# Values of the meta tokens from one stationary operand of 64 columns, in the bank of the first value tile

## The chip, the cores and the metric

The kernel runs on one core of a Trainium2 chip. The metric is the device time of one execution in microseconds, taken as the median over runs. A profiled execution has its own time and a trace with every instruction of the engines: TensorE (PE; its weight loads are listed as PEld), VectorE (DVE), ScalarE (ACT), GpSimd (POOL), and SyncE (SP), which issues DMAs.

## What is computed

One decoder layer on 256 tokens with 16 learned meta tokens ahead of them (272 keys). From the normalised input one projection gives queries, a latent of 256 numbers for each token, an indexer and gates. Each query attends to its top 68 keys. The part that matters here, cut from the reference:

```python
c_kv = rms_norm(c_kv, kv_norm_g[l])
q_lat = jnp.einsum('bthe,hce->bthc', q, w_uk)
...
sel = c_kv[batch_ix, idx]
s = jnp.einsum('bqhr,bqkr->bqhk', ql, sel).astype(jnp.float32) * (HEAD_DIM ** -0.5)
...
p = jax.nn.softmax(s, axis=-1).astype(sel.dtype)
return jnp.einsum('bqhk,bqkr->bqhr', p, sel)
...
o = jnp.einsum('bthc,hce->bthe', o_lat, w_uv)
```

The kernel makes keys (latent times w_uk) and values (latent times w_uv) for each of 16 heads instead, masks the keys that were not chosen, and multiplies. After the attention come the output projections, the merge with a pooling branch, and the MLP.

## The kernel before

Every fp32 factor is split into two parts, hi (rounded, made by ACT) and lo (the rest, made by DVE or, for half of some weights, by POOL). A product takes three matmuls: hi times hi, hi times lo, lo times hi. Weights stream in blocks; the cast of a block's weights (L239, ACT) and its lo parts (L242 on DVE and POOL) are written three blocks ahead of their matmuls. Every engine runs its instructions in the order of the program.

`kv_block(m)`, for m = 0 to 7, is one such weight block and makes keys and values of heads 2m and 2m+1. Eight of them are inserted among the blocks of the input projection; the text calls them blocks 0 to 7. Each made five PSUM banks of the pool `m` in turn: the keys of each head (`mm3`, L147 to L149, split by L112 on ACT and L113 on DVE), then the values of the meta tokens, of tokens 0 to 127 (v0) and of tokens 128 to 255 (v1), each with six matmuls (L626 to L628: two halves of the latent, three products). v0 and v1 are split by L112 and L113. The pool `m` has three banks, so the fourth and fifth users wait until the first and second have been read.

The values of the meta tokens are kept as four strips of 32 partitions in one tile `vm`: hi (L631, ACT), hi again, lo (L632, DVE), hi again (L635, two ACT copies behind L632). The probabilities of the meta tokens lie in the same way in `pm`: hi in partitions 0 to 15, lo in 32 to 47, hi in 64 to 79, zeros elsewhere (L700, L701, L703). One matmul of 128 partitions, L715, then adds the three products at once; the fourth strip of `vm` meets zeros.

The attention of a head is a queue of small steps, one popped ahead of each weight block: scores (`s1`, 6 matmuls, L147 to L149 on q and k), then `s4` (L715 and the products with v0 and v1) with the exponentials, then `s3` (transposes L692 to L697, then the splits into `pt` and `pm`) with the normalisation (L683, L684). A score step mostly stands right behind a kv block. Where a slab of output columns ends, four banks of the pool `g` (five banks) are emptied by ACT (L133) and DVE (L134), and the next slab's matmuls L305 need them.

Of the kernel before, what the change touches and what calls it, by code (L numbers as in the profile page):

```python
# [9 lines left out]
F32 = mybir.dt.float32  # L10
F32R = mybir.dt.float32r
AF = mybir.ActivationFunctionType
ALU = mybir.AluOpType
# [3 lines left out]
P = 128  # L17
D = 2048
KC = D // P
S = 256  # L20
NM = 16
# [50 lines left out]
def flat(slot):  # L72
    return slot.rearrange("p a b -> p (a b)")
# [4 lines left out]
def decoder_layer(ctx, tc, x, meta, g_mix, w_in, kv_g, ik_g, w_uk, w_uv, w_ao, w_pool,  # L78
                  pool_scale, w_po, w_out, g_mlp, w1, w2, g_fin, out):
    nc = tc.nc  # L80
    x, out, w_in, w_ao, w_po, w_out, w1, w2 = x[0], out[0], w_in[0], w_ao[0], w_po[0], w_out[0], w1[0], w2[0]
# [12 lines left out]
    ecst = early.enter_context(tc.tile_pool(name="ecst", bufs=1))  # L94
# [4 lines left out]
    slots = Slots(act, NSLOT, F32R, "r")  # L99
    plain = Slots(fpl, NPLAIN, F32, "f")  # L100
    V, A, T, G = nc.vector, nc.scalar, nc.tensor, nc.gpsimd
# [6 lines left out]
    def mbank():  # L108
        return pm.tile([P, 512], F32, tag="m", name="m")

    def split_psum(dst, ps, n, rows=P):
        A.copy(dst[:rows, 0, :n], ps)  # L112
        V.tensor_tensor(out=dst[:rows, 1, :n], in0=ps, in1=dst.bitcast(F32)[:rows, 0, :n], op=ALU.subtract)  # L113

    def split_sbuf(dst, src, n):
        A.copy(dst[:, 0, :n], src)
        V.tensor_tensor(out=dst[:, 1, :n], in0=src, in1=dst.bitcast(F32)[:, 0, :n], op=ALU.subtract)
# [28 lines left out]
    def mm3(ps, wh, wl, xh, xl, first, last):  # L146
        T.matmul(ps, wh, xh, start=first, stop=False)  # L147
        T.matmul(ps, wh, xl, start=False, stop=False)  # L148
        T.matmul(ps, wl, xh, start=False, stop=last)  # L149
# [41 lines left out]
    def add_unit(load, halves):  # L191
        u = {"load": load, "left": len(halves)}
        for src, shape, mm, pops in halves:
            blocks.append(Block(u, src, shape, mm, pops))
        return blocks[-len(halves)]
# [55 lines left out]
    def push(fn, ready=None):  # L251
        side.append((fn, ready))
# [134 lines left out]
        return hT[k], NM  # L387

    kvraw, ckv, qi, kw = {}, [], [], {}
    wn = [cst.tile([P, IH], F32, name=f"wn{t}") for t in range(2)]  # L390

    def split_heads(dst, ps):
# [22 lines left out]
    def push_kv_norm():  # L415
        env = {}

        def s0():
            kvf = kvraw["t"]
            for cc in range(2):  # L420
                V.tensor_tensor(out=kvf[:, cc, :], in0=kvf[:, cc, :], in1=rbc, op=ALU.mult)

        def s1():
            env["sq"] = plain.get()
            A.activation(flat(env["sq"]), flat(kvraw["t"]), AF.Square)

        def s2():
            ps = mbank()
            sq = env["sq"]
            for cc in range(2):  # L430
                T.matmul(ps[:, 0:L], ones, sq[:, cc, :], start=cc == 0, stop=cc == 1)
            env["r"] = plain.get()
            V.tensor_scalar(env["r"][:, 0, :], ps[:, 0:L], 1.0 / R, EPS, op0=ALU.mult, op1=ALU.add)

        def s2b():
            A.activation(env["r"][:, 0, :], env["r"][:, 0, :], AF.Sqrt)

        def s2c():
            V.reciprocal(env["r"][:, 0, :], env["r"][:, 0, :])

        def s3():
            kvf = kvraw["t"]
            for cc in range(2):
                V.scalar_tensor_tensor(out=kvf[:, cc, :], in0=kvf[:, cc, :], scalar=gcol[:, 40 + cc:41 + cc],
                                       in1=env["r"][:, 0, :], op0=ALU.mult, op1=ALU.mult)

        def s4():
            kvf = kvraw["t"]
            for cc in range(2):
                t = slots.get()  # L450
                split_sbuf(t, kvf[:, cc, :], L)
                ckv.append(t)
            for k in ("sq", "r"):
                plain.put(env[k])
            plain.put(kvraw["t"])

        for f in (s0, s1, s2, s2b, s2c, s3, s4):
            push(f)
# [144 lines left out]
    vP = {}  # L603

    def kv_block(m):
        def load(raw):
            for kind, w in ((0, w_uk), (1, w_uv)):
                nc.sync.dma_start(out=raw[:, kind * 512:(kind + 1) * 512].rearrange("p (a e) -> p a e", e=DH),
                                  in_=w[2 * m:2 * m + 2].rearrange("h (c p) e -> p (h c) e", p=P))

        def go(hi, lo):
            hi = hi.rearrange("p k (h c e) -> p k h c e", h=2, c=2)
            lo = lo.rearrange("p k (h c e) -> p k h c e", h=2, c=2)
            for h in range(2):
                ps = mbank()[:, 0:L]
                for c in range(2):
                    mm3(ps, hi[:, 0, h, c], lo[:, 0, h, c], ckv[c][:, 0, :], ckv[c][:, 1, :], c == 0, c == 1)
                kT[2 * m + h] = slots.get()
                split_psum(kT[2 * m + h], ps, L)
            vv = []  # L620
            for o, rows in ((0, NM), (NM, P), (NM + P, P)):
                ps = mbank()[:, 0:S]
                pv = ps.rearrange("p (h e) -> p h e", h=2)
                for c in range(2):
                    ch, cl = ckv[c][:, 0, o:o + P], ckv[c][:, 1, o:o + P]
                    T.matmul(pv, ch, hi[:, 1, :, c], start=c == 0, stop=False)  # L626
                    T.matmul(pv, ch, lo[:, 1, :, c], start=False, stop=False)
                    T.matmul(pv, cl, hi[:, 1, :, c], start=False, stop=c == 1)  # L628
                t = slots.get()
                if rows == NM:  # L630
                    A.copy(t[0:32, 0, 0:S], ps[0:32])  # L631
                    V.tensor_tensor(out=t[64:96, 0, 0:S], in0=ps[0:32], in1=t.bitcast(F32)[0:32, 0, 0:S],  # L632
                                    op=ALU.subtract)
                    for o in (32, 96):
                        A.copy(t[o:o + 32, 0, 0:S], ps[0:32])  # L635
                else:
                    split_psum(t, ps[0:rows, :], S, rows)
                vv.append(t)
            vP[m] = vv

        add_unit(load, [(lambda raw: raw[:, 0:1024].rearrange("p (k n) -> p k n", k=2), (2, 512), go, 0)])
        blocks[-1].split_late = True
        at, pops = KV_AT, 0
        while pops < 6 * m:
            pops += blocks[at].pops
            at += 1
        blocks.insert(at, blocks.pop())

    def push_attention():
# [36 lines left out]
        def s3(h):  # L686
            def go():
                sm, _ = env[h]
                f = flat(sm)
                pt = ptp.tile([P, 2, 384], F32R, tag="pt", name="pt")  # L690
                ps = mbank()
                T.transpose(ps[:, 0:P], f[:, NM:N0], ident)  # L692
                T.transpose(ps[:, P:2 * P], f[:, N0 + NM:N0 + NM + P], ident)
                T.transpose(ps[:, 2 * P:3 * P], f[:, N0 + NM + P:SC], ident)
                pz = mbank()
                T.transpose(pz[0:NM, 0:P], f[:, 0:NM], ident)
                T.transpose(pz[0:NM, P:2 * P], f[:, N0:N0 + NM], ident)  # L697
                split_psum(pt, ps[:, 0:384], 384)
                pm_ = pms[h % 2]
                A.copy(pm_[0:NM], pz[0:NM, 0:S])  # L700
                V.tensor_tensor(out=pm_[32:32 + NM], in0=pz[0:NM, 0:S], in1=pm_.bitcast(F32)[0:NM],  # L701
                                op=ALU.subtract)
                A.copy(pm_[64:64 + NM], pz[0:NM, 0:S])  # L703
                plain.put(sm)
                env[h] = pt
            return go
# [604 lines left out]
    for gi in range(4):  # L1311
        n = len(blocks)
# [75 lines left out]
    ps = mbank()  # L1388
# [66 lines left out]
```

## Time and profile before

| | |
|---|---|
| median of 3 runs | 1397.49 us (1397.42 to 1397.7) |
| profiled execution, own time | 1395.8 us |
| its span, first to last instruction | 1394.0 us |
| TensorE busy over the span | 1377.0 us, 99% |
| DVE, ACT, POOL busy | 1003.1, 782.5, 214.6 us |
| granted TensorE clock, mean | 0.998 |

Matmuls are pipelined: a row's duration runs to the end of its result, and the next matmul starts well before that. What a matmul costs is read from the distance between starts, and a wait from a larger distance and the note in brackets on who released it.

### The profile page before, as it was taken

To read this page: it belongs to the slowest core of one execution; us is meant where nothing else is said; L and a number is where in the kernel's file an instruction comes from. 1 tells how busy PE (TensorE), PEld (TensorE's weight loads), DVE (VectorE), ACT (ScalarE), POOL (GpSimd) and SP (SyncE) were. 2 spreads that over 40 slices of the span, in tenths; PEclk is the share of its full clock that TensorE was granted. 3 is DMA by queue.
4 is the path that set the end of the run, shared out by engine and by line. 5 is a ranking of instruction groups with operands and counts; after the bars stand their busy time and mean duration, and the time that the engine had idled before them with its cause. 6 is when DMAs were issued, how large, how long until landed. Compare 5 with 4: busy or idle time off the path is not lost.

```text
span 1394.0 us, 19873 instructions
## 1 busy us (share of the span) xinstructions
PE 1377.0 (99%) x7616; PEld 1187.9 (85%) x7616; DVE 1003.1 (72%) x1519; ACT 782.5 (56%) x1244; POOL 214.6 (15%) x176
## 2 busy tenths in 40 slices
PE   9999999999999999999999999999999999999997
PEld 8888888899988888888888888888888888788886
DVE  5768965565667857665567887679877797977994
ACT  5655466665555745454465566455655555545562
POOL 1055455454314000010000011000220002000000
PEclk9999999999999999999999999999999999999999
DMA  6554544434545554675555578645887458654562
GB/s 231 194 184 152 166 159 162 162 123 140 180 153 183 181 207 154 211 247 177 190 183 169 194 229 243 201 166 198 248 240 239 164 199 251 233 199 169 195 219 97
DMA packets 125999, 264.63 MB, mean 190 GB/s; under 512 B 5222, under 2 KB 16528, under 8 KB 125904
## 3 DMA queue, kind: packets, MB, share of 16 engines
q1 hardware_dynamic: 119440, 250.63, 52.6%
q0 software_dynamic: 5824, 11.65, 4.1%
q8 instruction: 59, 0.97, 0.3%
q10 hardware_dynamic: 640, 1.09, 0.2%
q14 instruction: 36, 0.29, 0.1%
HBM read 252.86 MB, written 2.10 MB: 183 GB/s over the span
## 4 chain that ended last, share of the span: by engine, by line
PE 82%; DVE 11%; DMA 3%; ACT 2%; issue 1%; POOL 0%; DVEq 0%; ACTq 0%; SPq 0%; POOLq 0%
PE g L305 34%; PE g L306 17%; DVE lo L244 3%; DMA raw<-in_w_mlp_out_dram 3%; PE g L335 3%; PE g L333 3%; PE g L334 3%; PE m L986 2%; PE m L988 2%; PE m L987 2%; PE g L147 2%; PE g L148 2%; PE g L149 2%; ACT hi L239 2%; PE g L987 2%; PE g L988 2%
## 5 line engine op out<-in xcount | busy, mean ns | idle before, releaser
L305 PE MATMUL g<-r,hi 128*128 128x512 f32 x2240 | 791.2, 396 | 1.3 <-DVE f L134 1.3
L239 ACT CAST hi<-raw 128x1024 fp32r<-128x1024 f32 (+1 forms) x441 | 454.9, 1046 | 352.3 <-PE g L305 227.0
L306 PE MATMUL g<-r,lo 128*128 128x256 f32 x2240 | 630.3, 281 | 0.0
L244 DVE TENSOR_TENSOR lo<-raw,hi 128x1024 fp32r<-128x1024 f32 (+1 forms) x349 | 422.8, 1221 | 232.0 <-ACT hi L239 230.7
L305 PEld LDWEIGHTS g<-r,hi 128*128 128x128 f32 x2240 | 421.1, 188 | 97.9 <-DVE f L134 2.5
L306 PEld LDWEIGHTS g<-r,lo 128*128 128x128 f32 x2240 | 422.9, 189 | 0.2
L242 POOL TENSOR_TENSOR lo<-raw,hi 128x512 fp32r<-128x512 f32 x92 | 153.4, 1674 | 207.3 <-ACT hi L239 146.0
L242 DVE TENSOR_TENSOR lo<-raw,hi 128x512 fp32r<-128x512 f32 x92 | 84.9, 923 | 72.1 <-ACT hi L239 72.1
L1096 POOL DMA_DIRECT2D w<-w x32 | 28.0, 1197 | 538.8 <-ACT w L1093 287.1
L986 PE MATMUL m<-hi,r 128*128 128x512 f32 x224 | 88.6, 396 | 0.0
L988 PE MATMUL m<-hi,r 128*128 128x512 f32 x224 | 88.2, 394 | 0.0
L987 PE MATMUL m<-lo,r 128*128 128x512 f32 x224 | 88.1, 393 | 0.0
L133 ACT COPY b<-g 128x256 f32<-128x256 f32 x148 | 54.6, 370 | 25.4 <-PE g L306 20.8
L987 PE MATMUL g<-lo,r 128*128 128x512 f32 x168 | 66.5, 396 | 2.2 <-DVE lo L244 1.8
L988 PE MATMUL g<-hi,r 128*128 128x512 f32 x168 | 66.3, 395 | 0.0
L986 PE MATMUL g<-hi,r 128*128 128x512 f32 x168 | 66.3, 395 | 0.0
L333 PE MATMUL g<-hi,r 128*128 128x512 f32 x160 | 64.4, 402 | 0.0
L335 PE MATMUL g<-hi,r 128*128 128x512 f32 x160 | 63.3, 396 | 0.0
L334 PE MATMUL g<-lo,r 128*128 128x512 f32 x160 | 62.5, 391 | 0.0
L125 ACT CAST r<-w 128x256 fp32r<-128x256 f32 x96 | 39.0, 407 | 41.3 <-DVE w L1191 27.9
L239 ACT CAST hi<-ta 128x1024 fp32r<-128x1024 f32 x28 | 29.4, 1050 | 55.2 <-DVE ta L1015 41.3
L147 PE MATMUL g<-r,hi 128*128 128x272 f32 (+4 forms) x192 | 56.8, 296 | 0.0
(252 smaller groups left out, 1799.1 us busy)
## 6 DMA issues: line engine op xcount, KB each, us to landing
raw<-in_w_mlp_in_dram SPq DMA_DIRECT2D x64, 1024.0 KB, 5.1
raw<-in_w_mlp_out_dram SPq DMA_DIRECT2D x64, 1024.0 KB, 5.3
raw<-in_w_in_dram SPq DMA_DIRECT2D x56, 1024.0 KB, 4.9
raw<-in_w_attn_o_dram SPq DMA_DIRECT2D x16, 1024.0 KB, 5.0
raw<-in_w_out_dram SPq DMA_DIRECT2D x16, 1024.0 KB, 5.1
raw<-in_w_pool_o_dram SPq DMA_DIRECT2D x8, 1024.0 KB, 5.0
w<-w POOLq DMA_DIRECT2D x32, 256.0 KB, 8.9
raw<-in_w_in_dram SPq DMA_DIRECT2D x8, 512.0 KB, 8.1
```

Source lines behind the costliest of these rows:

```text
L147: T.matmul(ps, wh, xh, start=first, stop=False)
L239: A.copy(hv, src)
L242: e.tensor_tensor(out=lv[:, kk], in0=src[:, kk], in1=hv.bitcast(F32)[:, kk], op=ALU.subtract)
L244: V.tensor_tensor(out=lv, in0=src, in1=hv.bitcast(F32), op=ALU.subtract)
L305: T.matmul(ps, wh, xt[:, :, o:o + S], start=f, stop=False)
L306: T.matmul(ps[:, 0], wl, xt[:, 0, o:o + S], start=False, stop=l)
L333: T.matmul(ps, xh, hi[:, kk], start=f, stop=False)
L334: T.matmul(ps, xh, lo[:, kk], start=False, stop=False)
L335: T.matmul(ps, xl, hi[:, kk], start=False, stop=l)
L986: T.matmul(ps, xh, wh, start=first, stop=False)
L987: T.matmul(ps, xh, wl, start=False, stop=False)
L988: T.matmul(ps, xl, wh, start=False, stop=last)
```

## The change

The latent of the meta tokens gets an operand of its own, `cmeta`: for each half of the latent 64 columns, 32 of hi and 32 of lo, copied once by DVE when the latent is split. The values of the meta tokens are then made by four matmuls with 64 stationary columns, two for each half of the latent (with hi and with lo of the weight): rows 0 to 31 of the result hold the product with the latent's hi, rows 32 to 63 that with its lo. The result lies in the second half of the bank whose first half holds v0, and its matmuls stand behind v0's split in the program. The four strips of `vm` are made after v1: hi, lo, hi of the latent's lo product, hi again. The fourth strip is now used, so `pm` gets its hi part a second time, in partitions 96 to 111: one more ACT copy for each head.

```diff
@@ -387,6 +387,7 @@
         return hT[k], NM
 
     kvraw, ckv, qi, kw = {}, [], [], {}
+    cmeta = ecst.tile([P, 2, 64], F32R, name="cmeta")
     wn = [cst.tile([P, IH], F32, name=f"wn{t}") for t in range(2)]
 
     def split_heads(dst, ps):
@@ -449,6 +450,7 @@
             for cc in range(2):
                 t = slots.get()
                 split_sbuf(t, kvf[:, cc, :], L)
+                V.tensor_copy(cmeta[:, cc].rearrange("p (a n) -> p a n", a=2), t[:, :, 0:32])
                 ckv.append(t)
             for k in ("sq", "r"):
                 plain.put(env[k])
@@ -617,9 +619,10 @@
                     mm3(ps, hi[:, 0, h, c], lo[:, 0, h, c], ckv[c][:, 0, :], ckv[c][:, 1, :], c == 0, c == 1)
                 kT[2 * m + h] = slots.get()
                 split_psum(kT[2 * m + h], ps, L)
-            vv = []
-            for o, rows in ((0, NM), (NM, P), (NM + P, P)):
-                ps = mbank()[:, 0:S]
+            vm, vv = slots.get(), []
+            for o in (NM, NM + P):
+                bank = mbank()
+                ps = bank[:, 0:S]
                 pv = ps.rearrange("p (h e) -> p h e", h=2)
                 for c in range(2):
                     ch, cl = ckv[c][:, 0, o:o + P], ckv[c][:, 1, o:o + P]
@@ -627,16 +630,19 @@
                     T.matmul(pv, ch, lo[:, 1, :, c], start=False, stop=False)
                     T.matmul(pv, cl, hi[:, 1, :, c], start=False, stop=c == 1)
                 t = slots.get()
-                if rows == NM:
-                    A.copy(t[0:32, 0, 0:S], ps[0:32])
-                    V.tensor_tensor(out=t[64:96, 0, 0:S], in0=ps[0:32], in1=t.bitcast(F32)[0:32, 0, 0:S],
-                                    op=ALU.subtract)
-                    for o in (32, 96):
-                        A.copy(t[o:o + 32, 0, 0:S], ps[0:32])
-                else:
-                    split_psum(t, ps[0:rows, :], S, rows)
+                split_psum(t, ps, S)
                 vv.append(t)
-            vP[m] = vv
+                if o == NM:
+                    pz = bank[:, S:2 * S]
+                    zv = pz.rearrange("p (h e) -> p h e", h=2)[0:64]
+                    for c in range(2):
+                        T.matmul(zv, cmeta[:, c], hi[:, 1, :, c], start=c == 0, stop=False)
+                        T.matmul(zv, cmeta[:, c], lo[:, 1, :, c], start=False, stop=c == 1)
+            A.copy(vm[0:32, 0, 0:S], pz[0:32])
+            V.tensor_tensor(out=vm[64:96, 0, 0:S], in0=pz[0:32], in1=vm.bitcast(F32)[0:32, 0, 0:S], op=ALU.subtract)
+            A.copy(vm[96:128, 0, 0:S], pz[32:64])
+            A.copy(vm[32:64, 0, 0:S], pz[0:32])
+            vP[m] = [vm] + vv
 
         add_unit(load, [(lambda raw: raw[:, 0:1024].rearrange("p (k n) -> p k n", k=2), (2, 512), go, 0)])
         blocks[-1].split_late = True
@@ -700,7 +706,8 @@
                 A.copy(pm_[0:NM], pz[0:NM, 0:S])
                 V.tensor_tensor(out=pm_[32:32 + NM], in0=pz[0:NM, 0:S], in1=pm_.bitcast(F32)[0:NM],
                                 op=ALU.subtract)
-                A.copy(pm_[64:64 + NM], pz[0:NM, 0:S])
+                for o in (64, 96):
+                    A.copy(pm_[o:o + NM], pz[0:NM, 0:S])
                 plain.put(sm)
                 env[h] = pt
             return go
```

TensorE's order at block 0, before: the end of the meta group, v0 and the start of v1, with the semaphores that an instruction waits for in brackets (r_113 and r_114 are the two halves of the latent, hi and lo the weights).

```order
L628 MATMUL m<-hi,r_114 128x256
L626 MATMUL m<-hi,r_113 128x256 [waits DVE_49]
L627 MATMUL m<-lo,r_113 128x256
L628 MATMUL m<-hi,r_113 128x256
L626 MATMUL m<-hi,r_114 128x256
L627 MATMUL m<-lo,r_114 128x256
L628 MATMUL m<-hi,r_114 128x256
L626 MATMUL m<-hi,r_113 128x256 [waits DVE_49]
```

TensorE's order at the same place in the changed program: the end of v0, the meta matmuls, the start of v1.

```order
L630 MATMUL m<-lo,r_114 128x256
L631 MATMUL m<-hi,r_114 128x256
L639 MATMUL m<-hi,cmeta 64x256 [waits DVE_49]
L640 MATMUL m<-lo,cmeta 64x256
L639 MATMUL m<-hi,cmeta 64x256
L640 MATMUL m<-lo,cmeta 64x256
L629 MATMUL m<-hi,r_113 128x256
L630 MATMUL m<-lo,r_113 128x256
```

The two waits for DVE ahead of v0 and v1 are gone, and there is one ahead of the first meta matmul. The count it names is reached when the DVE half of v0's split (L113) has ended; the key splits stand ahead of that on DVE. The score matmul behind the block waited for the second L635 and now waits for the copy of the first keys.

ACT's order at block 0, before: the key copies (r_129, r_130), the strip copies (r_131), the copies of v0 and v1 (r_132, r_109), the next weights' cast.

```order
L112 CAST r_129<-m 128x272 [waits PE_49]
L112 CAST r_130<-m 128x272 [waits PE_49]
L631 CAST r_131<-m 32x256 [waits PE_49]
L635 CAST r_131<-m 32x256 [waits DVE_49]
L635 CAST r_131<-m 32x256
L112 CAST r_132<-m 128x256 [waits PE_49]
L112 CAST r_109<-m 128x256 [waits PE_49]
L239 CAST hi<-raw 128x1024 [waits Pool_49]
```

ACT's order at the same place in the changed program.

```order
L112 CAST r_129<-m 128x272 [waits PE_49]
L112 CAST r_130<-m 128x272 [waits PE_49]
L112 CAST r_132<-m 128x256 [waits PE_49]
L112 CAST r_109<-m 128x256 [waits PE_49]
L641 CAST r_131<-m 32x256 [waits DVE_49]
L643 CAST r_131<-m 32x256 [waits DVE_49]
L644 CAST r_131<-m 32x256
L239 CAST hi<-raw 128x1024 [waits Pool_49]
```

The three strip copies moved behind the copies of v0 and v1; the first of them waits for v0's split on DVE, the second for the strip's subtraction. That subtraction moved on DVE in the same way, behind that of v1.

## Rows read from the trace of the kernel before

**Rows 1.** Busy us by stage: stretch, length, PE, PEld, DVE, ACT, POOL, clock, DMA.

```profile
165.00:400.00 235.00, 230.21 (x1585) 211.82 (x1584) 146.33 (x294) 143.03 (x307) 100.74 (x62) 1.00 0.47 154
```

**Rows 2.** Waits of TensorE's weight loads, whole run: total us, times, longest us.

```profile
PEld g L987 <- DVE lo L244: 4.8, 6, 1.8
PEld m L1376 <- issue: 3.2, 16, 0.3
PEld m L626 <- DVE r L113: 2.9, 3, 1.3
PEld m L147 <- ACT r L635: 1.8, 4, 0.5
PEld m L715 <- ACT pm L703: 1.3, 2, 0.7
```

**Rows 3.** Timeline, block 4: start us, duration us, engine, line [idle before <- releaser].

```profile
277.18 0.28 PE L628 MATMUL m<-hi,r 128*128 128x256 f32 x1
277.49 0.36 ACT L631 CAST r<-m 32x256 fp32r<-32x256 f32 x1 [0.32 <-PE m L628]
277.89 0.42 DVE L632 TENSOR_TENSOR r<-m,r 32x256 fp32r<-32x256 f32 x1 [0.24 <-ACT r L631]
277.89 0.28 PE L628 MATMUL m<-hi,r 128*128 128x256 f32 x1
279.13 0.34 PE L147 MATMUL m<-r,r 128*128 128x144 f32 x1 [0.24 <-ACT r L635]
279.63 2.01 ACT L239 CAST hi<-raw 128x1024 fp32r<-128x1024 f32 x2
279.94 0.39 PE L305 MATMUL g<-r,hi 128*128 128x512 f32 x1
```

**Rows 4.** Timeline, block 0.

```profile
169.00 0.42 DVE L632 TENSOR_TENSOR r<-m,r 32x256 fp32r<-32x256 f32 x1
171.05 0.39 PE L305 MATMUL g<-r,hi 128*128 128x512 f32 x1
```

**Rows 5.** Timeline, block 1; x2 marks two instructions printed as one row.

```profile
194.08 0.65 ACT L112 CAST r<-m 128x272 fp32r<-128x272 f32 x2
194.48 0.79 DVE L113 TENSOR_TENSOR r<-m,r 128x272 fp32r<-128x272 f32 x2 [1.35 <-ACT r L112]
194.97 0.39 PE L626 MATMUL m<-hi,r 128*128 128x256 f32 x1 [0.63 <-DVE r L113]
195.20 0.28 PE L627 MATMUL m<-lo,r 128*128 128x256 f32 x1
197.34 0.39 PE L305 MATMUL g<-r,hi 128*128 128x512 f32 x1
```

**Rows 6.** Timeline of TensorE, score matmuls with no wait ahead of them.

```profile
350.34 0.23 PE L147 MATMUL m<-r,r 128*128 128x144 f32 x1
351.05 0.39 PE L305 MATMUL g<-r,hi 128*128 128x512 f32 x1
```

**Rows 7.** Timeline, end of block 3 and the slab end behind it.

```profile
249.86 0.39 PE L305 MATMUL g<-r,hi 128*128 128x512 f32 x1
250.76 2.01 ACT L239 CAST hi<-raw 128x1024 fp32r<-128x1024 f32 x2
254.17 0.41 DVE L134 TENSOR_TENSOR f<-g,b 128x256 f32<-128x256 f32 x1
254.63 0.50 PE L305 MATMUL g<-r,hi 128*128 128x512 f32 x1 [0.41 <-DVE f L134]
```

**Rows 8.** Timeline, slab end behind block 4.

```profile
286.00 0.41 DVE L134 TENSOR_TENSOR f<-g,b 128x256 f32<-128x256 f32 x1
287.07 0.28 PE L147 MATMUL g<-r,hi 128*128 128x258 f32 x1
```

**Rows 9.** Timeline, transposes with 128 and with 16 stationary columns.

```profile
188.77 0.27 PE L694 MATMUL m<-ident,f 128*128 128x128 f32 x1
188.88 0.27 PE L696 MATMUL m<-ident,f 128*16 128x128 f32 x1
```

## The prediction

> **What bounds the kernel now.** I read the busy times by stage first. In the 235 us in which keys, values and attention are made, TensorE is busy 230.21 us, at granted clock 1.00 [rows 1]; so only what TensorE issues and what it waits for counts there. Then the list of what its weight loads waited for [rows 2]. Two entries belong to the blocks that the change rewrites: in blocks 0 to 2 the first matmul of v0 (the values of tokens 0 to 127) waits for the split of the first keys (L113, 3 times), and in blocks 4 to 7 the score matmul behind the block waits for the copies of the meta strip (L635, 4 times). Third, the timeline of block 4, which blocks 5 to 7 repeat [rows 3], and of blocks 0, 1 and 3, where the neighbours differ [rows 4, 5, 7]. Block 2 repeats block 1.
>
> **What is removed and added on TensorE.** Six matmuls of the meta group become four, in 8 blocks: 16 fewer. Matmuls of 256 columns start 0.118 us apart (six from 277.18 to 277.89 [rows 3]), so 16 x 0.118 = 1.9 us would be saved if nothing waited. No row here has a 64-column stationary operand in this stage. The bounds for one are 0.11 us, the spacing between transposes with 128 and with 16 stationary columns [rows 9], and 0.118; I take 0.118, since the moving operand is what stays at 256.
>
> **The added wait.** The four meta matmuls now write the second half of the bank of v0, and stand behind the split of v0 in the program. In the changed order the first of them waits for DVE, and the count that it waits for is that of the DVE half of v0's split. So per block TensorE stops between v0 and meta until ACT has copied v0 and DVE has subtracted. All TensorE work behind it queues: the meta matmuls, v1, the scores, then the next weight block. How long, from block 4: v0 takes the place of the old meta group, its last matmul starts at 277.18, ACT begins at 277.49, DVE at 277.89 and ends at 278.31 [rows 3]; there it was the strip's subtraction that took 0.42, and I take the same for v0's, since the two key subtractions, a little wider, take 0.79 together [rows 5]. The first of those ends at 194.48 + 0.395 = 194.88 and releases a matmul that starts at 194.97, 0.09 later; the one behind it starts 0.23 after it instead of 0.118 [rows 5]. So meta starts at 278.40, v1 at 278.40 + 0.23 + 3 x 0.118 = 278.98, the scores at 279.69. Their wait for the strip copies is gone (the order shows them waiting for a key copy long done), so they take 0.71, as where they start without a wait [rows 6], not the 0.81 from 279.13 to 279.94. The next weight block starts at 280.40 against 279.94: **+0.46**, for blocks 4 to 7 **+1.84**.
>
> Block 3 runs like block 4, 28.87 us earlier (ACT's cast 250.76 against 279.63), but has no scores behind it and waited for nothing: its next weight block goes from 249.86 to 279.69 - 28.87 = 250.82, **+0.96**.
>
> Block 0: DVE is late, and v0's subtraction comes where the strip's stood, 169.00 to 169.42 [rows 4]. Meta 169.51, v1 170.09, scores 170.80, next weights 171.51 against 171.05: **+0.46**.
>
> Blocks 1 and 2: ACT is late. The change puts one more copy of the probabilities' meta strip (0.36, as L631 [rows 3]) into ACT ahead of the key copies, which move from 194.08 to 194.44; the two key subtractions then end at 194.84 + 0.79 = 195.63 [rows 5], v0's at 196.07, meta starts at 196.17, v1 at 196.74, scores at 197.45, next weights at 198.16 against 197.34: **+0.82** each, 1.64. The same extra copy delays v0's bank here by 0.36; this lies under the wait just counted.
>
> The eight blocks: 1.84 + 0.96 + 0.46 + 1.64 = **+4.9 us**.
>
> **What is queued behind it on ACT and DVE.** The strip's four operations now follow the copy and subtraction of v1. In block 4: v1's last matmul starts at 279.57, ACT copies it from 279.88 (0.36) and the strip (0.36); DVE subtracts v1 (to 280.69) and the strip (to 281.11); ACT's last two copies end at 281.86. The weight cast L239 behind them moves from 279.63 to 281.87, +2.24 on ACT and, through it, on DVE, where TensorE moved by 0.46. Mostly this is hidden: a cast is for weights three blocks on. It isn't where an output slab ends right behind the block, since TensorE then needs banks that ACT and DVE empty behind these casts. Behind block 3 TensorE already waits for such a DVE addition (L134) at 254.63 [rows 7]; DVE's 254.17 becomes 256.41 and TensorE's 254.63 becomes 256.87, +2.24, that is **+1.28** over the 0.96. Behind block 4 the addition ends at 286.41; with 2.24 on it at 288.65, and the matmul that needs its bank, at 287.07 [rows 8], would come at 287.53: **+1.22**. The bounds are 0 and these values, for DVE has idle time in the stage (146.33 busy of 235 [rows 1]); I take the upper ends, since the casts' subtractions stand ahead of these additions on DVE. The other blocks' slabs end further on.
>
> **The rest.** The extra probability copy is ACT work, 16 x 0.36 = 5.8 us of 143.03 busy [rows 1], hidden by TensorE except where L715 waits for it, twice [rows 2]: **+0.72**, and 0 if cover appeared. Two small DVE copies into cmeta lie in the index stage, where TensorE waits for no split of the latent: 0; uncovered, under 2 x 0.42. No DMA and no instruction on POOL or SP moves.
>
> **Sum:** 4.9 + 1.28 + 1.22 + 0.72 = +8.1 us. The profiled execution took 1395.8 us (span 1394.0), so the sum gives 1403.9 for such a run. The median of the runs, 1397.49, lies 1.7 above it; on the median the forecast is **1405.6 us**.
>
> **Rivals.**
> *The evacuations stay hidden.* DVE's casts behind blocks 3 and 4 shorten or slip, and only the 4.9 and 0.72 remain: 1403.1. For it: DVE is busy only 62% of the stage. Against: TensorE already waits at 254.63.
>
> *A change of stationary width costs time of its own.* From 16 rows to 128 and back TensorE's loads sit idle for "issue", 16 times, 3.2 us in all [rows 2]; from 128 to 16 columns they don't, starts are 0.11 apart [rows 9]. If 64 columns behaved as the 16 rows, the way in is covered by the wait and the way out costs 8 x 0.2 = 1.6: 1407.2. The Trainium skill's page "TensorEngine Tiling (Array Packing)", section "Key Properties", says that changing the tiling mode drains TensorE; by it this rival would hold if 64 columns count as another mode. The row on 16 columns speaks against that, but it is a transpose and no matmul.
>
> *Later slack gives it back.* TensorE waits 4.8 us for split weights in the last stage (L987) [rows 2]. If those splits ran on a clock of their own, a later TensorE would wait that much less: 8.1 - 4.8 = +3.3, 1400.8. Against: the casts take their buffers from TensorE's own progress, so they come later too.
>
> *Faster: the new wait is over before TensorE gets there.* It decides at one place, the first meta matmul. If that needed only the key splits and not v0's, block 4 would run meta at 277.30, v1 at 277.77, scores at 278.48, next weights at 279.19, -0.75, four times -3.0; block 3 -0.24; in block 0 v1 at about 168.7 (0.3 before the strip's subtraction) and next weights at 170.20, -0.85; blocks 1 and 2 v1 at 195.33 and next weights at 196.85, -0.49 each; with +0.72: -4.4, **1393.1**. It needs the meta bank's readers to be done 1.1 us earlier than the rows allow. The trace of before never shows a matmul into a bank that ACT or DVE still reads. The Trainium skill's page "PSUM — Partial Sum Buffer", section "PSUM bank collisions raise a hardware error", says that two engines may not use one bank in the same partitions at once, and asks for semaphores by bank; it speaks against this change and for the wait, and no run here shows such a collision. Without the page, the wait stands in the changed order all the same.
>
> **How the numbers follow.** Forecast 59%, evacuations hidden 15%, width costs 12%, later slack 8%, faster 6%. The predicted time is the first, 1405.6. The 8 in 10: the low end lies near the later-slack case, 1401.0; the high end above the width case by the spacing's and restarts' uncertainty (8 x 0.15 = 1.2): 1408.5. About 0.2%, 2.8 us, is what a measurement of this kernel can tell from no change. Faster by more: the last rival, 0.06. Within: half of later slack and a little of the hidden evacuations, 0.05. Slower: the rest, 0.89.
>
> **What would show it.** Right: a wait of TensorE or its weight load on L113 before the first meta matmul in all 8 blocks, about 1.1 us in blocks 3 to 7; no wait of the scores on a strip copy; four meta matmuls 0.12 apart behind the first; a longer wait for L134 behind block 3 (some 1.7 us) and a new one behind block 4; L715's two waits 0.36 longer; the stages after 400 us as long as before. Wrong: no wait before the meta matmuls; an idle "issue" before v1; a shorter last stage.

## The result and the profile after

The changed kernel takes 1404.99 us in the median (1403.43 to 1406.92, 6 runs) against 1397.49 us before: ratio 1.0059, 95% interval 1.0049 to 1.0069, slower by about 8 us. The forecast was 1405.6. The profiled execution has a span of 1403.0 us against 1394.0, and its granted clock is 0.998 in both.

What TensorE's weight loads waited for, in the whole run, after (engine, line, what was waited for, us in total, times, longest); it answers to [rows 2]:

```profile
PEld m L639 <- DVE r L113: 10.6, 8, 1.9
PEld g L994 <- DVE lo L244: 5.3, 6, 2.6
PEld g L305 <- DVE f L134: 3.8, 4, 2.1
...
PEld m L722 <- ACT pm L710: 2.4, 2, 1.3
...
PEld g L147 <- DVE f L134: 0.8, 2, 0.7
PEld m L629 <- ACT pm L710: 0.8, 2, 0.4
```

L639 is the first meta matmul; it waits in all eight blocks for the DVE half of a split. The two old entries, L626 for L113 and L147 for L635, are gone. L305 waited 2.5 us before, L722 (L715 before) 1.3, and two entries are new, the last two.

The busy times by stage after, for [rows 1] (length, PE, PEld, DVE, ACT, POOL, then the granted clock, DMA share, GB/s):

```profile
165.00:400.00 235.00, 222.07 (x1520) 203.84 (x1520) 148.72 (x288) 145.06 (x316) 96.34 (x61) 0.99 0.45 149
```

TensorE is busy 8.1 us less in these 235 us. The clock reads 0.99 instead of 1.00; that was not in the forecast and is taken up below.

Block 4 after, TensorE, ACT and DVE (start, length, engine, line, operation, output and input, idle time before it and its releaser); compare [rows 3]:

```profile
282.07 0.28 PE L631 MATMUL m<-hi,r 128*128 128x256 f32 x1
...
282.38 0.37 ACT L112 CAST r<-m 128x256 fp32r<-128x256 f32 x1 [0.32 <-PE m L631]
282.79 0.42 DVE L113 TENSOR_TENSOR r<-m,r 128x256 fp32r<-128x256 f32 x1 [0.25 <-ACT r L112]
...
283.27 0.33 PE L639 MATMUL m<-hi,cmeta 128*64 128x256 f32 x1 [0.92 <-DVE r L113]
...
283.44 0.28 PE L640 MATMUL m<-lo,cmeta 128*64 128x256 f32 x1
...
283.79 0.28 PE L629 MATMUL m<-hi,r 128*128 128x256 f32 x1
...
284.50 0.23 PE L147 MATMUL m<-r,r 128*128 128x144 f32 x1
...
285.21 0.39 PE L305 MATMUL g<-r,hi 128*128 128x512 f32 x1
```

The chain is the forecast one: v0's last matmul at 282.07, ACT's copy, DVE's subtraction to 283.21, the meta group at 283.27, v1 at 283.79, the scores without a wait at 284.50, the next weights at 285.21. TensorE stands still for 0.92 us.

Where TensorE's 9.0 us went, from the distance between the starts of neighbouring blocks, after minus before (so 28.44 us from block 0 to block 1 after, 26.66 before, +1.78):

| place | after minus before, us |
|---|---|
| block 0 | +1.78 |
| blocks 1, 2 | +0.64, +0.60 |
| block 3 and the slab end behind it | +0.87, +1.31 |
| block 4 and the slab end behind it | +0.37, +1.01 |
| blocks 5, 6, 7 | +0.35, +0.35, +0.35 |
| the two waits of L722 | +1.13 |
| the last stages | +0.55 |

These add up to 9.3; block 0 began 0.3 us earlier. The start of block 0 lies between 164.3 and 165.6 in the traces of this document, with nearly the same program ahead of it, so all that follows compares distances. The slab end behind block 3 after, for [rows 7]:

```profile
255.71 2.00 ACT L239 CAST hi<-raw 128x1024 fp32r<-128x1024 f32 x2
...
259.55 0.50 PE L305 MATMUL g<-r,hi 128*128 128x512 f32 x1 [1.74 <-DVE f L134]
```

### The profile page after: what moved, and what is told of

The parts are those of the page before. It is cut to its first block, busy times and chain, and to the rows that moved or that the text cites. A ratio compares the mean times of both kernels' runs of the same rounds, so it can differ in the third digit from the quotient of the medians.

```text
span 1403.0 us, 19859 instructions
## 1 busy us (share of the span) xinstructions
PE 1376.8 (98%) x7600; PEld 1186.9 (85%) x7600; DVE 1010.5 (72%) x1521; ACT 788.9 (56%) x1260; POOL 210.5 (15%) x176
## 4 chain that ended last, share of the span: by engine, by line
PE 81%; DVE 11%; DMA 3%; ACT 2%; issue 1%; POOL 0%; DVEq 0%; ACTq 0%; SPq 0%; POOLq 0%
PE g L305 33%; PE g L306 17%; DVE lo L244 3%; DMA raw<-in_w_mlp_out_dram 3%; PE g L335 3%; PE g L333 3%; PE g L334 3%; PE m L993 2%; PE m L995 2%; PE m L994 2%; PE g L147 2%; PE g L148 2%; PE g L149 2%; ACT hi L239 2%; PE g L994 2%; DVE lo L242 2%
## 5 line engine op out<-in xcount | busy, mean ns | idle before, releaser
L305 PE MATMUL g<-r,hi 128*128 128x512 f32 x2240 | 792.4, 396 | 2.6 <-DVE f L134 2.6
L305 PEld LDWEIGHTS g<-r,hi 128*128 128x128 f32 x2240 | 421.7, 188 | 99.4 <-DVE f L134 3.8
L242 POOL TENSOR_TENSOR lo<-raw,hi 128x512 fp32r<-128x512 f32 x92 | 149.2, 1630 | 220.7 <-ACT hi L239 146.3
L242 DVE TENSOR_TENSOR lo<-raw,hi 128x512 fp32r<-128x512 f32 x92 | 93.3, 1015 | 67.8 <-ACT hi L239 67.8
L133 ACT COPY b<-g 128x256 f32<-128x256 f32 x148 | 54.5, 371 | 26.5 <-PE g L306 19.9
L147 PE MATMUL g<-r,hi 128*128 128x272 f32 (+4 forms) x192 | 57.1, 297 | 0.4 <-DVE f L134 0.4
```

The source lines that it names most:

```text
L242: e.tensor_tensor(out=lv[:, kk], in0=src[:, kk], in1=hv.bitcast(F32)[:, kk], op=ALU.subtract)
L305: T.matmul(ps, wh, xt[:, :, o:o + S], start=f, stop=False)
```

## The experiments

Each ran beside the kernel before on one chip; ratios are to that kernel, with 95% intervals. The chip was one for e1 to e4, another for e5 to e8, another for e9 to e11 and another for e12, so runs of different groups are compared by their ratios and by distances in the traces. A distance runs from a block's first matmul to the next block's, or, for "the blocks with their scores", to the first one behind the scores; unless another run is named it is compared with the kernel before. Each trace shows one execution.

**e1, the meta matmuls ahead of v0's split.** One part is undone, the place behind the split; bank, operand and extra copy stay.

```diff
+                if o == NM:
+                    pz = bank[:, S:2 * S]
+                    ... (the four matmuls)
                 t = slots.get()
                 split_psum(t, ps, S)
                 vv.append(t)
-                if o == NM:
-                    ...
```

> The changed kernel with one thing moved: the four meta matmuls stand right behind the last matmul of v0 and ahead of v0's split, in the same bank. TensorE then has nothing to wait for at the meta group; four PSUM banks per block, the 64-column operand and the extra probability copy stay. Theory (the wait of the first meta matmul for the DVE half of v0's split is the cause): no wait on L113 before the meta group; v1 right behind it, waiting at most for the first key split; against the kernel before, block 0 -0.9, blocks 1 and 2 -0.5 each, block 3 -0.24, blocks 4 to 7 -0.76 each, the evacuations behind blocks 3 and 4 +1.2 each (the strip's operations still stand ahead of the weight cast, about 1 us late), L722's two waits +1.1: 1395.8 us; granted clock 1.00 through block 0. Rival (the width of the stationary operand, the extra copy or the place of the strip's operations is the cause, and the wait only hides it): 1403 to 1405.

Measured: 1395.76 us, ratio 0.9994 (0.9986 to 1.0003). No wait is left at the meta group; v1 waits 0.60 us for the first key split in block 0 and 0.15 in blocks 1 and 2. The blocks with their scores take 0.84 less (block 0), 0.47 and 0.48 (1, 2), 0.28 (3) and 0.75 to 0.79 (4 to 7), 5.2 us in all: the rival of the prediction that said "faster" had these sizes right, and its condition is what the changed kernel lacked. Only 1.9 us of them are the sixteen matmuls (16 x 0.118); the rest comes from the old waits on L113 (2.9 us of weight loads before, 1.7 now) and L635 (1.8, gone). In block 0 the clock stays at 1.00. What remains are the waits behind the blocks: +1.34 behind block 3, and +1.66 behind block 4, where the changed kernel had +1.01:

```profile
250.06 2.00 ACT L239 CAST hi<-raw 128x1024 fp32r<-128x1024 f32 x2
...
253.91 0.50 PE L305 MATMUL g<-r,hi 128*128 128x512 f32 x1 [1.75 <-DVE f L134]
```

So the place of four matmuls behind one split is worth about 9 us, and everything else in the change comes to nearly nothing in sum: what the blocks gain, the waits behind them and the copies take back.

**e2, a bank of its own for the meta group.** The matmuls stay behind the split.

```diff
-                    pz = bank[:, S:2 * S]
+                    pz = mbank()[:, 0:S]
```

> The changed kernel with a bank of its own for the meta group, so five banks per block as before; the meta matmuls stay behind v0's split in the program, with the 64-column operand. Theory (it is the shared bank that makes the wait): the wait on L113 goes; block 0 -0.4, blocks 1 and 2 -0.1 each, block 3 -0.24, blocks 4 to 7 -0.76 each, the two evacuations +1.2 each and L722 +1.1 stay, 1397.2 us, the same as before. Rival (the place of the matmuls behind the split in the program, or the width, makes the wait): 1403 to 1405.

Measured: 1398.16 us, ratio 1.0006 (0.9997 to 1.0014). The wait on L113 remains in blocks 0 to 2 alone, where it is that for the first keys' bank. The blocks with their scores take 0.43 less than before (block 0), 0.05 (1, 2), 0.22 (3) and 0.70 to 0.73 (4 to 7), 3.6 us in all. It is the shared bank that makes the wait. The Trainium skill's page "PSUM — Partial Sum Buffer", section "PSUM bank collisions raise a hardware error", asks for the ordering by bank. e2 shows what it costs here when a second group is put into a bank that is being emptied: the eight blocks take 3.8 us more than before in the changed kernel, its fall of the clock left out, and 3.6 less in e2, together 7.4 us. No run here shows a collision.

**e3, the strip's four operations behind the next weight cast.**

```diff
-            A.copy(vm[0:32, 0, 0:S], pz[0:32])
-            ... (the other three)
+            deferred.append(strips)
...
             convert(i + 3)
+        while deferred:
+            deferred.pop()()
```

> The changed kernel with the strip's four ACT and DVE operations put behind the weight cast that follows the block, instead of ahead of it; TensorE's program stays, the wait of the meta group too. Theory (the delayed cast, by the strip's operations behind v1, makes TensorE wait for the evacuations behind blocks 3 and 4): those two waits shorten by about 1.2 and 1.0 us, the rest stays, the fall of the granted clock in block 0 too: 1402.7 us. Rival (the evacuations are late for another reason, with TensorE itself): 1405, unchanged.

Measured: 1402.63 us, ratio 1.0039 (1.0027 to 1.0052). The time is what the theory said, by luck: the way is not. Behind block 4 the wait shrank (the distance by 0.62) and the second wait behind block 3 went, but the first did not. ACT and TensorE behind block 3:

```profile
253.95 2.00 ACT L239 CAST hi<-raw 128x1024 fp32r<-128x1024 f32 x2
255.84 0.35 ACT L645 CAST r<-m 32x256 fp32r<-32x256 f32 x1
257.90 0.36 ACT L647 CAST r<-m 32x256 fp32r<-32x256 f32 x1 [1.70 <-DVE r L646]
...
258.66 1.29 ACT L133 COPY b<-g 128x256 f32<-128x256 f32 x4
...
259.54 0.50 PE L305 MATMUL g<-r,hi 128*128 128x512 f32 x1 [1.70 <-DVE f L134]
```

The cast is early now, but the strip stands between it and the slab's copies L133, and ACT waits 1.70 us there for the strip's subtraction. The strip was moved past the cast and not past what TensorE waits for.

**e4, the kernel before with the extra probability copy alone.**

```diff
+                A.copy(spare[0:NM], pz[0:NM, 0:S])
                 A.copy(pm_[64:64 + NM], pz[0:NM, 0:S])
```

> The kernel before, with one more ACT copy of 16 x 256 per head (from the same bank, into a tile that nobody reads) ahead of the last copies of the probabilities' meta strip: the ACT work that the change adds there, alone. Theory: hidden in most places, but the two waits of L715 become 0.4 to 0.55 longer each (+1.1), and the keys' copies in blocks 1 and 2 come 0.36 later (+0.7): 1399.3 us. Rival: hidden everywhere, 1397.5 us; second rival: it costs in every block, 16 x 0.36 = 5.8 us, 1403.

Measured: 1397.61 us, ratio 1.0006 (0.9997 to 1.0015); that doesn't tell +1.8 from 0. The trace does. TensorE's weight loads:

```profile
PEld m L717 <- ACT pm L705: 2.0, 2, 1.1
...
PEld m L627 <- ACT pm L705: 0.8, 2, 0.4
```

Blocks 1 and 2 take 0.39 and 0.38 more, TensorE stands still before the last products for 0.74 more in two waits (0.64 before, 1.38 now), the other blocks nothing: +1.5 us of 5.8 us of ACT's work.

**e5, e1 with the strip behind the whole next weight block**, thus behind the slab's copies too.

```diff
+        held = deferred[:]
+        deferred.clear()
         b.mm(b.hi, b.lo)
+        for fn in held:
+            fn()
```

> The kernel of e1 (meta matmuls ahead of v0's split) with the strip's four operations moved behind the whole weight block that follows the keys and values, thus behind the evacuation of an output slab that ends there; in e3 they still stood ahead of those copies (L133). Theory (it is the strip's place ahead of the additions L134 that makes TensorE wait behind blocks 3 and 4): the wait of 1.75 us behind block 3 falls to 0.5 or less, the one of 1.1 behind block 4 goes, 1395.8 - 3.3 = 1392.5 us. Rival (the evacuations are late for another reason, as e3 could suggest): 1395.8, as e1.

Measured: 1397.45 us, ratio 0.9998 (0.9989 to 1.0007), 5 us above the theory. Behind block 3 it did what it should: the first wait is gone, the distance is 1.54 us shorter than in e1. But the strip is now ahead of other slabs. Behind block 4, on ACT and TensorE:

```profile
279.53 0.36 ACT L645 CAST r<-m 32x256 fp32r<-32x256 f32 x1
282.82 0.36 ACT L647 CAST r<-m 32x256 fp32r<-32x256 f32 x1 [2.94 <-DVE r L646]
...
284.54 0.91 ACT L133 COPY b<-g 128x256 f32<-128x256 f32 x3
...
285.75 0.39 PE L147 MATMUL g<-r,hi 128*128 128x258 f32 x1 [0.59 <-DVE f L134]
...
287.17 0.39 PE L147 MATMUL g<-r,hi 128*128 128x260 f32 x1 [0.44 <-DVE f L134]
```

Block 4's distance with its slab end grew by 0.49 against e1, block 0's by 1.15. Block 0's all arises at the slab end behind it, between 185.3 and 187.8: a wait of 0.45 for L134 at 186.69, and wider spacing of the matmuls next to it. Another 1.36 came behind block 7, 0.8 of it up to the last products and 0.6 in the last stages; its cause was not traced. Neither the theory nor the rival had said that other slabs would be late.

**e6, e5 without the extra copy.** The strip's low rows are added on DVE instead.

```diff
-                for o in (64, 96):
-                    A.copy(pm_[o:o + NM], pz[0:NM, 0:S])
+                A.copy(pm_[64:64 + NM], pz[0:NM, 0:S])
...
+                V.tensor_tensor(out=vm[64:96, 0, 0:S], in0=pz[32:64], ..., op=ALU.add)
```

> The kernel of e5 without the extra probability copy: the 32 rows of the meta values' low part (weights times the low half of the latent) are added on DVE to the strip's residual rows, so that rows 96 to 111 of the probabilities' strip are not needed; one DVE addition more per block, 16 ACT copies less. Theory (the extra copy costs what e4 showed, 0.4 in blocks 1 and 2 each and 0.7 at the two waits of L722): 1392.5 - 1.5 = 1391.0 us. Rival (with other work out of the way the copy is hidden): 1392.5, as e5.

Measured: 1397.95 us, ratio 1.0003 (0.9995 to 1.0012). Block 2 takes 0.37 less than in e5, as the copy would give, but the longer DVE strip makes the slab behind block 0 later (a wait of 1.65 us, 0.45 in e5). In the trace, DVE work put where a slab waits costs more than the ACT work that it saved; the two times are not apart beyond their intervals.

**e7, the order of e1 in block 0 alone.**

```diff
-                split_psum(t, ps, S)
+                if o == NM and m > 0:
+                    split_psum(t, ps, S)
...
+                if o != NM or m == 0:
+                    split_psum(t, ps, S)
```

> The changed kernel with the meta matmuls ahead of v0's split in block 0 alone; blocks 1 to 7 as in the changed kernel. Theory (the pause of 2.0 us in block 0 brings the granted clock down, and the fall costs about 1.3 us beside the pause's own 1.2 or so): block 0 takes 2.6 us less, 1402.4 us, and the clock stays at 1.00 there. Rival (the clock falls in block 0 for another reason): clock falls all the same, 1403.8 us.

Measured: 1404.36 us, ratio 1.0053 (1.0041 to 1.0065); the times can't separate 1402.4 from 1403.8. In the traces block 0's distance is 2.62 us shorter than in the changed kernel (-0.84 against +1.78). Block 0 by stretches of 2 us, the changed kernel first, then e7 (the third number from the end is the granted clock):

```profile
170.00:172.00 2.00, 2.00 (x13) 1.90 (x12) 0.84 (x2) 0.84 (x3) 0.00 (x0) 0.67 0.03 8
172.00:174.00 2.00, 2.00 (x8) 1.71 (x8) 0.37 (x1) 1.96 (x4) 0.32 (x1) 0.50 0.00 0
```

```profile
170.00:172.00 2.00, 2.00 (x14) 1.74 (x13) 0.61 (x2) 1.29 (x3) 0.00 (x0) 1.00 0.00 0
172.00:174.00 2.00, 2.00 (x14) 1.74 (x13) 1.23 (x2) 2.00 (x3) 1.44 (x1) 1.00 0.00 0
```

In the changed kernel the clock is at its lower level, 0.50 (1.2 GHz), from about 170.7 to 174, behind a pause in which no matmul started for 2.02 us; TensorE is busy throughout, with 8 matmuls where e7 has 14.

**e8, longer pauses in blocks 4 to 7.**

```diff
                 t = slots.get()
+                for _ in range({4: 2, 5: 3, 6: 4, 7: 6}.get(m, 0) if o == NM else 0):
+                    A.copy(spare[:, 0:S], ps)
                 split_psum(t, ps, S)
```

> The changed kernel with the pause before the meta matmuls made longer in blocks 4 to 7: 2, 3, 4 and 6 more ACT copies of v0's bank (into a tile that nobody reads) ahead of v0's split, about 0.31 us each, so that the first meta matmul starts some 1.8, 2.1, 2.4 and 3.1 us behind the matmul before it. Theory (a pause of about 2 us or more brings the granted clock to half for some microseconds, whatever the block): the clock falls behind the pauses of blocks 6 and 7, perhaps 5; 1405.0 + 4.7 + two or three times 1.3 = 1412.3 to 1413.6 us. Rival (the fall belongs to block 0, not to the length of the pause): no fall in blocks 4 to 7, 1409.7 us.

Measured: 1413.8 us, ratio 1.0115 (1.0102 to 1.0129), near the theory's 1413.6, and the theory is wrong all the same: the longer pauses themselves cost 5.6 us and not 4.7, and the falls came elsewhere. The first meta matmul in blocks 0, 4, 5, 6 and 7:

```profile
169.31 0.33 PE L642 MATMUL m<-hi,cmeta 128*64 128x256 f32 x1 [1.77 <-DVE r L113]
...
284.12 0.33 PE L642 MATMUL m<-hi,cmeta 128*64 128x256 f32 x1 [1.60 <-DVE r L113]
...
315.52 0.33 PE L642 MATMUL m<-hi,cmeta 128*64 128x256 f32 x1 [2.00 <-DVE r L113]
...
346.27 0.33 PE L642 MATMUL m<-hi,cmeta 128*64 128x256 f32 x1 [2.40 <-DVE r L113]
...
377.49 0.33 PE L642 MATMUL m<-hi,cmeta 128*64 128x256 f32 x1 [3.21 <-DVE r L113]
```

Behind none of these five does the clock fall, not even behind 3.49 us from start to start. It fell behind the wait at the end of block 3 (2.03 us) and once in the last stages (2.25 us). The rival is wrong too: block 0, with the same instructions and the same pause as in the changed kernel, kept its clock. This gives the fall's price in block 0: the distance to block 1 is +0.26 here and +1.78 in the changed kernel, so 1.52 us.

**e9, e1 with the strip between the splits of v0 and v1**, its three ACT copies together.

```diff
                 split_psum(t, ps, S)
                 vv.append(t)
+                if o == NM:
+                    A.copy(vm[0:32, 0, 0:S], pz[0:32])
+                    ... (the other two copies, then the subtraction)
```

> The kernel of e1 (meta matmuls ahead of v0's split) with the strip's operations between the splits of v0 and v1, its three ACT copies together and the DVE subtraction last, where e1 has them behind v1 and e5 had them behind the next weight block. ACT then takes the weight cast up about 1.0 us behind the last matmul of v1, as in the kernel before, where it is 2.4 us in e1. Theory (the lag of the cast behind the block makes the waits for the additions L134): the wait behind block 3 falls from 1.75 to about 0.45, the one of 1.1 us behind block 4 goes, and none appears behind block 0 as in e5: 1395.8 - 3.0 = 1392.8 us. Rival (wherever the strip stands, some slab's evacuation is late by it): 1395.8 to 1397.5.

Measured: 1394.91 us, ratio 0.9986 (0.9977 to 0.9995). No new wait behind block 0, 0.5 us less than in e1 behind block 3 and 0.5 behind block 4, where 1.3 and 1.1 were expected:

```profile
249.91 2.00 ACT L239 CAST hi<-raw 128x1024 fp32r<-128x1024 f32 x2
...
253.77 0.50 PE L305 MATMUL g<-r,hi 128*128 128x512 f32 x1 [1.25 <-DVE f L134]
```

The lag of the cast behind the start of the next weight block (248.15) is 1.76 us, where before it is 0.90: the strip's first copy waits 0.49 until DVE is done with v0 in the same bank. With the other runs this gives a rule for the slab end behind block 3, when nothing else stands between the cast and the slab: lags of 0.90 (before), 1.76 (e9), 2.26 (after) and 2.27 (e1) gave waits of 0.41, 1.25, 1.74 and 1.75. Here the wait is the lag less 0.5.

**e10, e9 with all ACT copies of the probabilities' strip ahead of DVE's subtraction.**

```diff
+                for o in (64, 96):
+                    A.copy(pm_[o:o + NM], pz[0:NM, 0:S])
                 V.tensor_tensor(out=pm_[32:32 + NM], ...)
-                for o in (64, 96):
-                    A.copy(pm_[o:o + NM], pz[0:NM, 0:S])
```

> The kernel of e9 with the three ACT copies of the probabilities' meta strip together ahead of DVE's subtraction, which stood between the first and the other two, so that ACT need not wait for DVE there. Theory (the two waits of L722 hang on ACT's copies, which wait 1.95 us for DVE): these waits shorten by 0.4 to 0.7 each, and the keys' copies in blocks 1 and 2 come earlier: 1392.8 - 1.3 = 1391.5 us. Rival (DVE's subtraction is itself the last and ends as late as before): 1392.8, as e9.

Measured: 1392.3 us, ratio 0.9972 (0.9961 to 0.9983), 2.6 us less than e9, where the theory had 1.3. Before the last products:

```profile
390.10 0.73 ACT L710 CAST pm<-m 16x256 fp32r<-16x256 f32 x2
391.38 0.41 DVE L711 TENSOR_TENSOR pm<-m,pm 16x256 fp32r<-16x256 f32 x1
391.85 0.19 PEld L724 LDWEIGHTS m<-pm,r 128*128 128x128 f32 x1 [0.33 <-DVE pm L711]
```

ACT's copies lie behind no wait, and L724's two weight loads wait 0.5 us in all, where they waited 2.0 in e9. Blocks 1 and 2 are 0.5 and 0.4 us shorter. At the slab end at 428.10 TensorE now waits 0.88 for L134, 0.42 in e9, so about 0.46 is lost again there.

**e11, e9 with 128 columns in the meta operand.** The 64 columns stand there twice; the upper half of the result is not read.

```diff
-    cmeta = ecst.tile([P, 2, 64], F32R, name="cmeta")
+    cmeta = ecst.tile([P, 2, 128], F32R, name="cmeta")
```

> The kernel of e9 with the meta tokens' stationary operand filled up to 128 columns (the 64 columns twice; the upper 64 rows of the result are not read), so that no matmul of the block has another width than 128. Theory (a width of 64 columns costs nothing by itself): as e9, 1392.8 us, and the matmuls behind the meta group follow 0.12 apart in both. Rival (changing the width costs 0.2 us per block): 1.6 us less than e9.

Measured: 1394.78 us, ratio 0.9990 (0.9981 to 0.9999), the time of e9. The way into and out of the meta group in block 4:

```profile
276.55 0.28 PE L632 MATMUL m<-hi,r 128*128 128x256 f32 x1
276.67 0.27 PE L637 MATMUL m<-hi,cmeta 128*128 128x256 f32 x1
...
277.02 0.28 PE L638 MATMUL m<-lo,cmeta 128*128 128x256 f32 x1
277.14 0.28 PE L630 MATMUL m<-hi,r 128*128 128x256 f32 x1
```

0.12 apart on both sides; in e9, with 64 columns, the starts are 0.11 to 0.12 apart too (v0's last at 246.87, meta from 246.99 to 247.33, v1 at 247.45). All blocks agree with e9 within 0.03 us. The distance from block 3 to block 4 is 1.57 longer, with the clock at 0.50 from about 254.7 to 258.1, nearly the same price of a fall as in e8.

**e12, e10 with block 3's strip alone behind the next weight block.**

```diff
+                    if m == 3:
+                        deferred.append(strips)
+                    else:
+                        strips()
```

> The kernel of e10 with the strip's operations of block 3 alone moved behind the weight block that follows it, as in e5; the other blocks as in e10. By the runs so far the first wait behind block 3 was 0.5 us shorter than the lag of the weight cast (L239) behind the block's last matmul: lags of 0.90, 1.76, 2.27 and 2.26 us gave waits of 0.41, 1.25, 1.75 and 1.74. Theory (this rule holds): the cast comes 0.47 us behind the block, the first wait of 1.26 us goes, the second of 0.45 stays or grows a little, no new wait appears: 1392.3 - 1.2 = 1391.1 us. Rival (the strip then makes the next slab late, as behind block 0 in e5): 1392.3, as e10.

Measured: 1391.23 us, ratio 0.9963 (0.9949 to 0.9976).

```profile
247.50 2.00 ACT L239 CAST hi<-raw 128x1024 fp32r<-128x1024 f32 x2
...
252.80 0.50 PE L305 MATMUL g<-r,hi 128*128 128x512 f32 x1 [0.47 <-DVE f L134]
```

The cast's lag is 0.47, the first wait is gone, only the second is left, and the distance is 1.29 us shorter than in e10. The rule of e9 held at the one place where it was used ahead of a run. This kernel is 5 us faster than the one before and, by the ratios, 13 us faster than the changed one; the idea of the change, one operand of 64 columns and four banks, is all in it.

## Why the prediction was right, and where it was not

**The new wait: right in kind, a little too long.** It appears at all eight places. Blocks 4 to 7 cost 0.35 to 0.37 each and not 0.46: the first meta matmul comes 0.06 behind DVE's end and the second 0.17 behind the first, where the forecast had 0.09 and 0.23 from the matmuls behind the key splits. Block 3 cost 0.87 (forecast 0.96), blocks 1 and 2 0.64 and 0.60 (0.82 each). Without a fall of the clock block 0 cost 0.26 (e8; forecast 0.46). In sum about 3.8 us (0.26 + 0.64 + 0.60 + 0.87 + 0.37 + 0.35 + 0.35 + 0.35) where the forecast was 4.9. e1 and e2 show that split and shared bank are both needed for it.

**The evacuations: right in size, and the cause narrower than told.** +1.31 behind block 3 (forecast 1.28) and +1.01 behind block 4 (forecast 1.22, though the two times it names, 288.65 and 287.53, are 1.12 apart). The step by which the strip's operations delay the cast, and the cast the additions, holds behind block 3: e9 and e12 put numbers on it. But e3 and e5 show that the strip can delay the additions without the cast, by standing directly ahead of them.

**L715's extra copy: too small.** +1.13 instead of +0.72. Of it 0.74 is the copy (e4). The other 0.38 lies at the first of the two waits and goes with the strip's place: TensorE's weight loads wait 2.4 us there in all five kernels that have the strip right behind v1 (after, e1, e2, e7, e8), and 2.0, as in e4, where it stands behind the cast (e3) or ahead of v1's split (e9, e11). e10 shows what was behind both waits: ACT's last copies stood behind DVE's subtraction. The copy's share in blocks 1 and 2 that the forecast took, 0.36 each, is the 0.39 and 0.38 of e4.

**The clock: missing.** The prediction had no term for it. In the profiled execution one fall cost 1.5 us of the 9.0, and it made up for what the forecast's waits were too long; so far the nearness of 9.0 to 8.1 is luck. Without it the terms of the forecast measure 3.8 + 2.3 + 1.1 = 7.2 us, where 8.1 were forecast. The medians, 7.5 us apart, depend little on it, for the kernel before loses clock in other executions too: the mean granted clock is 0.9963 over the six runs of the changed kernel, and 0.9965 to 0.9973 over the runs of the kernel before beside e1 to e12.

**The last stages: not as long as before, but +0.55.** The wait for split weights there went from 4.8 to 5.3 us in all [rows 2]; "later slack" gave nothing back. In the fourteen traces, whose programs are the same there, this wait is 4.8 to 6.5 us, so it is not shown that the change made the 0.55.

**The rivals.** Width: falls by e11. The Trainium skill's page "TensorEngine Tiling (Array Packing)", section "Key Properties", says that a change of tiling mode drains TensorE; if 64 columns are such a change, these starts at 0.11 to 0.12 us show no price for it. Hidden evacuations: fall, by the waits of 1.74. Faster: its condition was named rightly, "If that needed only the key splits and not v0's", and e1, which fulfils it in the program's order instead, has the block times that it gave. e1 came to 1395.8 and not to 1393.1 because the rival had left out the waits behind blocks 3 and 4 (+1.34 and +1.66).

## What to carry to other kernels

Before a second accumulation group is put into a bank, see in the program's order whether its first matmul stands behind the emptying of the first group: here that alone cost 9 us, and writing the four matmuls ahead of the split gave it back without another bank. When work is moved off the path on ACT or DVE, look for the next thing in that queue that TensorE needs: in e3 and e5, moving it past one such instruction only put it ahead of another. Here a saving of matmuls was worth its time only where nothing small and late, like the strip and the copies of the probabilities, stood between the block and the next slab.

## What the hardware showed that was not expected

The granted clock can fall to 0.50 behind a single pause of TensorE of about 2 us, in an otherwise full stage. It cost 1.52 us in block 0 and 1.47 and 1.57 behind block 3 (e8, e11); in e2, where it overlaps with the next wait there, 1.06 (+2.40 against e1's +1.34). Whether it falls isn't settled by the pause's length: in the traces of the fourteen kernels, outside the first 140 us, TensorE paused 24 times for over 1.7 us from one matmul's start to the next. Eight of these pauses, of 2.02 to 2.47 us, were followed by a fall, sixteen, of 1.80 to 3.49 us, were not, and one fall came behind 1.53 us (e11). The same instructions in the same place did one in one trace and the other in another: the clock fell in block 0 of the changed kernel and not of e8, and behind block 3 in e8 and not in the changed kernel or e7. What decides it stays open; for reading traces it means that distances of single executions can differ by 1.5 us without a difference in the instructions.
